# Two small buffers requested first and one mask padded, in a four-branch encoder trunk on one core

## The chip, the cores and the metric

The kernel runs on one core of one Trainium2 chip. The metric is device time in microseconds, lower is better: 2187.64 us before the change, the median of 3 runs (2186.35 to 2188.82).

## The reference

Two inputs of 512 rows by 1024 channels, a prompt and a sample, go independently through the same trunk of two layers. One layer, cut to what matters:

```python
xn = _rms_norm(x, norm_g)
h = xn @ w_in                                   # 1024 -> 8096 columns
h_a, h_b, h_c, h_d, z, mg = _split_cols(h, [A_IN, B_IN, C_IN, D_IN, GATE_IN, MERGE_IN])
ys = [_mla_mixer(h_a, ...), _axial_gqa_mixer(h_b, ...), _sink_window_mixer(h_c, ...), _dilated_mixer(h_d, ...)]
merged = jnp.zeros_like(x)
for i in range(4):
    yi = ys[i] * jax.nn.silu(z[..., i * 256:(i + 1) * 256])
    gi = jax.nn.sigmoid(mg[..., i * D_MODEL:(i + 1) * D_MODEL])
    merged = merged + gi * (yi @ w_branch[i])
return x + merged @ w_out
```

The four mixers are a latent attention (A) and a grouped-query attention (B), both over all 512 positions, a window attention (C) and a dilated one (D). A last RMSNorm ends the trunk. Everything is in float32.

## The kernel before

**Layout of the work.** Activations lie channel-major: a tile has 128 partitions (channels) and a row of T = 512 float32 values (positions), 2048 bytes, in each partition. Four passes run one after the other: layer 0 for prompt and sample, then layer 1 for both. In each pass TensorE multiplies weight tiles of 128x128, which it loads (the page's PEld), by activation tiles, which it streams: a matmul "mm<-xn,wh 128x512" streams one 512-value row of each partition of a tile `xn` against weights of `wh`.

**Three products for one.** Each float32 operand is split in a high part (a rounded copy made on ScalarE) and a low part (the difference, made on VectorE). `mm3` (lines 121 to 124) issues three matmuls: weights high by activation high, high by low, low by high. `project` (line 126) does that over the eight tiles of 128 channels, 24 matmuls for one output tile. The normalised input is in eight buffers `xn0` to `xn7`, the gated branch outputs in `y`, and the queries, keys, latents and the scaled merged sum in `qk`; each of these holds the high row and behind it the low row, 2 x 2048 bytes. `ph` holds a high or a low part of the softmax weights, 2048 bytes. Weights arrive in `wr` and are split into `wh` and `wl` by `piece` (lines 99 to 119).

**Stages of a pass.** The list `steps` sets the program's order: dilated branch D, latents, gate projections `G`, the heads of A, projections and heads of B, branch D's merge `BR`, window branch C, then the merges `M` of A, B and C (each 24 matmuls that stream `xn` and 6 that stream `y` for one output tile). Last comes the output projection with `wo`, which streams eight `qk` tiles (`ms`): 192 matmuls of 128x512 in each of the first three passes, and the same in halves of 256 columns in the fourth. A planner that walks the program with its own clock orders the instructions of each engine, so that matmuls of the merges stand between those of the attention heads.

**Where buffers lie.** All of SBUF's buffers come from one pool through `new(tag, ...)` (line 39). A tag has `bufs` slots; the first request of a tag reserves them, directly behind the tag requested before it, each rounded up to a multiple of 32 bytes. The region begins at byte 16512 of each partition, which is 128 past a multiple of 256. The offsets in the program before the change follow by adding up the sizes in the order of the first requests:

| tags in order of first request | bytes each, slots | first byte | beyond a multiple of 256 |
|---|---|---|---|
| `ident`, `vecs`, `ones`, `heads` | 512, 256, 512, 512 | 16512 | 128 |
| `ms` | 64 x 2 | 18304 | 128 |
| `s`, `wr`, `wh`, `wl` | 8192 x 2, 2560 x 3, x 4, x 4 | 18432 | 0 |
| `qk` | 4096 x 8 | 62976 | 0 |
| `rx`, `rs`, `cos`, `sin`, `rstd` | 2048 x 2, x 3, 2048, 2048, 64 x 4 | 95744 | 0 |
| `nw` | 64 x 2 | 110336 | 0 |
| `lr`, `u` | 2048 x 2, x 2 | 110464 | 128 |
| `xn0` to `xn7` | 4096 each | 118656 | 128 |
| `bcos`, `bsin`, `atab`, `band`, `tri`, `band4` | 2048 x 3, 1536 x 2, 512 | 151424 | 128 |
| `blk` | 128 | 161152 | 128 |
| `v`, `th`, `z`, `mr`, `yf` | 2048 x 4, x 2, x 2, x 4, x 1 | 161280 | 0 |
| `ph` | 2048 x 6 | 187904 | 0 |
| `rc` | 64 x 2 | 200192 | 0 |
| `y` | 4096 x 3 | 200320 | 128 |
| `mg4` to `mg7`, `mg0` to `mg3` | 2048 each | 212608 | 128 |

`nw` is the scratch of the reciprocal square root (`rsqrt`, line 142), `rc` that of the softmax denominators (`gate`, line 301), and `blk` is the smallest mask of the dilated branch, 32 columns, loaded once in `load_tabs` (line 93) and read in `dilated_pair` (line 460). `ident` is streamed by the transposes of `flip` (line 268).

Of the kernel before, what the change touches and what calls it, by code (L numbers as in the profile page):

```python
# [7 lines left out]
F32 = mybir.dt.float32  # L8
# [5 lines left out]
P = 128  # L14
# [14 lines left out]
def trunk(ctx, tc, x0, x1, wp, wr, wu, wg, wb, wm, wo, vec, rope, msk, eye, y0, y1):  # L29
# [9 lines left out]
    def new(tag, shape, dt=F32, bufs=1):  # L39
        uid[0] += 1  # L40
        return sb.tile(shape, dt, tag=tag, name=f"{tag}_{uid[0]}", bufs=bufs)

    def bank(tag, bufs):
        uid[0] += 1
        return pp.tile([P, T], F32, tag=tag, name=f"{tag}_{uid[0]}", bufs=bufs)
# [15 lines left out]


    ident = new("ident", [P, P])
    vecs = new("vecs", [P, vec.shape[1]])

    def vcol(l, j):
        c = l * 24 + j
        return vecs[:, c : c + 1]

    ones = new("ones", [P, P])  # L70
    nc.vector.memset(ones, 1.0)
    heads = new("heads", [P, P])
# [4 lines left out]
    tabs = {}  # L77

    def load_tabs(names=None):
        for n, name in enumerate(("cos", "sin", "bcos", "bsin", "atab")):  # L80
            if name not in tabs and (names is None or name in names):
                tabs[name] = new(name, [P, T])
                nc.sync.dma_start(out=tabs[name], in_=rope[n])
        if names is not None:
            return
        nc.sync.dma_start(out=ident, in_=eye)
        tabs["band"] = new("band", [P, 384])
        nc.sync.dma_start(out=tabs["band"], in_=msk[:, 0:384])
        tabs["tri"] = new("tri", [P, 384])
        nc.sync.dma_start(out=tabs["tri"], in_=msk[:, 384:768])  # L90
        tabs["band4"] = new("band4", [P, P])
        nc.sync.dma_start(out=tabs["band4"], in_=msk[:, 768:896])
        tabs["blk"] = new("blk", [P, 32])
        nc.sync.dma_start(out=tabs["blk"], in_=msk[:, 896:928])


# [438 lines left out]
    def begin(xin):  # L535

        nc.scalar.dma_start(out=vecs, in_=vec)
        warm = new("ms", [P, 16], F32, 2)
        act(out=warm, in_=ones[:, 0:16], func=AF.Exp)
        src = wp[0, T_D + 6 * 1]  # L540
        early = [new("s", [P, 4 * T], F32, 2) for _ in range(2)]
        xt = [early[k // 4][:, (k % 4) * T : (k % 4 + 1) * T] for k in range(NK)]
        xg, pieces, acc = [], [], None
        for k in range(NK):
            nc.sync.dma_start(out=xt[k], in_=xin[:, k, :])
            if k % 4 == 0:
                pieces.append(piece(src[k // 4], 512))
            x = new("qk", [P, 2, T], F32R, 8)
            act(out=x[:, 0, :], in_=xt[k], func=AF.Copy, scale=vcol(0, k))
            stt(out=x[:, 1, :], in0=xt[k], scalar=vcol(0, k), in1=f(x[:, 0, :]), op0=ALU.mult, op1=ALU.subtract)  # L550
            xg.append(x)
            acc = squares(acc, xt[k], k)
        load_tabs(("cos", "sin"))
        bc = rstd([acc], ones, DM, "lr")
        ct, st = new("u", [P, T], F32, 2), new("u", [P, T], F32, 2)
        xn = normalise(0, xt, bc, True)
        tt(out=ct, in0=tabs["cos"], in1=bc, op=ALU.mult)
        tt(out=st, in0=tabs["sin"], in1=bc, op=ALU.mult)
        return xn, (xg, pieces, ct, st, bc)

    def layer(l, q_, xin, last_out, xn, ahead, early=None):
# [12 lines left out]
        def proj_d(g):  # L574
            nonlocal early
            xg, pieces, ct, st_, bc = early or (xn, None, tabs["cos"], tabs["sin"], None)
            p0 = ptile(T_D + 6 * g, xg, pieces)
            p1, p2 = [ptile(T_D + 6 * g + n, xg) for n in (1, 2)] if early else [None, None]
            if early:
                load_tabs()  # L580
            qs = [pack_q(rotary(p0, (0, P), ct, st_))]
            x = rotary(p1 or ptile(T_D + 6 * g + 1), (0, P), ct, st_)
            k1 = pack_k(x, 0, True)
            k4 = pack_k(x, 64)
            ps = p2 or ptile(T_D + 6 * g + 2)
            vt = new("rs", [P, T], F32, 3)
            if early:
                tt(out=inner(vt[64:128]), in0=blocks(ps[64:128]), in1=blocks(bc[64:128]), op=ALU.mult)
            else:
                nc.scalar.copy(out=inner(vt[64:128]), in_=blocks(ps[64:128]))  # L590
            x = rotary(ps, (0, 64), ct, st_)
            early = None
            k16 = pack_k(x, 0)
            v1 = pack_v(flip(vt, (64, 128)))
            qs.append(pack_q(rotary(ptile(T_D + 6 * g + 3), (0, P), tabs["cos"], tabs["sin"])))
            qs.append(pack_q(rotary(ptile(T_D + 6 * g + 4), (0, P), tabs["cos"], tabs["sin"])))
            ps = ptile(T_D + 6 * g + 5)
            vt = new("rs", [P, T], F32, 3)
            nc.scalar.copy(out=vt, in_=ps)
            vp = flip(vt, (0, P))  # L600
            v4 = pack_v(vp[:, :, 0:64])
            v16 = pack_v(vp[:, :, 64:128])
            return qs, [k1, k4, k16], [v1, v4, v16]
# [383 lines left out]
```

## Time and profile before

| | before |
|---|---|
| median of 3 runs | 2187.64 us |
| the profiled execution's own time | 2186.45 us |
| its span, first to last instruction | 2184.7 us |
| mean granted TensorE clock | 0.985 |
| TensorE busy | 2120.6 us, 97%, 9550 matmuls |
| VectorE busy | 1795.1 us, 82% |
| ScalarE busy | 1280.7 us, 59% |
| GpSimd busy | 411.2 us, 19% |
| weight loads busy (beside the matmuls) | 1722.1 us, 79% |
| DMA | 369.76 MB, 169 GB/s on average |

A group of instructions is told by line, engine, operation, its tiles (output<-inputs, the streamed tile first and the weights second) and its shape. The duration of a matmul runs from its start until its last result is out; the next one begins before that. How fast TensorE really goes is therefore read from the distance between the starts of two matmuls that follow each other, and not from the durations. The timeline gives these starts to 0.01 us.

### The profile page before, as it was taken

To read this page: it belongs to the slowest core of one execution; us is meant where nothing else is said; L and a number is where in the kernel's file an instruction comes from. 1 tells how busy PE (TensorE), PEld (TensorE's weight loads), DVE (VectorE), ACT (ScalarE), POOL (GpSimd) and SP (SyncE) were. 2 spreads that over 40 slices of the span, in tenths; PEclk is the share of its full clock that TensorE was granted. 3 is DMA by queue.
4 is the path that set the end of the run, shared out by engine and by line. 5 is a ranking of instruction groups with operands and counts; after the bars stand their busy time and mean duration, and the time that the engine had idled before them with its cause. 6 is when DMAs were issued, how large, how long until landed. Compare 5 with 4: busy or idle time off the path is not lost.

```text
span 2184.7 us, 28862 instructions
## 1 busy us (share of the span) xinstructions
PE 2120.6 (97%) x9550; PEld 1722.1 (79%) x9550; DVE 1795.1 (82%) x3113; ACT 1280.7 (59%) x2167; POOL 411.2 (19%) x145
## 2 busy tenths in 40 slices
PE   7999999999999999999999998999899999999998
PEld 5887778878888778888888776888688887788887
DVE  8999999987478998785379999999866889997725
ACT  6746675444565767553366466754456757675434
POOL 0032313220013221220002222122200232122200
PEclk9999999999999999999999999999899999999999
DMA  6543444556754445556754434455466544455565
GB/s 213 169 145 120 141 141 163 175 186 210 240 165 145 139 138 159 162 191 212 245 179 155 139 117 134 156 166 177 161 226 223 152 152 135 145 158 164 179 207 185
DMA packets 189798, 369.76 MB, mean 169 GB/s; under 512 B 21328, under 2 KB 30032, under 8 KB 188880
## 3 DMA queue, kind: packets, MB, share of 16 engines
q1 hardware_dynamic: 181152, 351.11, 50.0%
q10 hardware_dynamic: 8496, 16.81, 2.3%
q8 instruction: 75, 1.23, 0.2%
q14 instruction: 75, 0.61, 0.1%
HBM read 273.99 MB, written 93.85 MB: 168 GB/s over the span
## 4 chain that ended last, share of the span: by engine, by line
PE 88%; DVE 8%; issue 1%; DMA 1%; ACT 1%; SPq 0%; DVEq 0%; ACTq 0%
PE mm L122 26%; PE mm L123 26%; PE mm L124 25%; PE so L343 1%; PE so L342 1%; PE ss L351 1%; DVE ph L140 1%; PE ss L352 1%; DMA s<-x 1%; DVE wl L115 1%; PE mi L268 1%; PE ss L124 1%; PE ss L123 1%; PE ss L447 1%; PE ss L122 1%
## 5 line engine op out<-in xcount | busy, mean ns | idle before, releaser
L123 PE MATMUL mm<-xn,wh 128*128 128x512 f32 x1992 | 788.5, 396 | 5.9 <-DVE xn L524 5.9
L122 PE MATMUL mm<-xn,wh 128*128 128x512 f32 x1992 | 791.3, 397 | 1.4 <-ACT xn L523 1.0
L124 PE MATMUL mm<-xn,wl 128*128 128x512 f32 x1992 | 788.7, 396 | 0.0
L110 ACT CAST wh<-wr 128x512 fp32r<-128x512 f32 (+1 forms) x596 | 387.1, 651 | 412.5 <-PE mm L123 302.0
L123 PEld LDWEIGHTS mm<-xn,wh 128*128 128x128 f32 x1992 | 376.3, 189 | 90.7 <-DVE xn L524 6.2
L122 PEld LDWEIGHTS mm<-xn,wh 128*128 128x128 f32 x1992 | 376.0, 189 | 88.8 <-ACT xn L523 1.4
L124 PEld LDWEIGHTS mm<-xn,wl 128*128 128x128 f32 x1992 | 376.1, 189 | 85.8 <-issue 1.0
L291 POOL PARTITION_ALL_REDUCE mr<-mr x64 | 239.2, 3737 | 512.2 <-DVE mr L347 265.8
L286 POOL PARTITION_ALL_REDUCE mr<-mr x64 | 129.8, 2029 | 985.3 <-DVE mr L470 577.5
L115 DVE TENSOR_TENSOR wl<-wr,wh 128x512 fp32r<-128x512 f32 (+2 forms) x304 | 247.2, 815 | 40.2 <-ACT wh L110 36.5
L140 DVE TENSOR_TENSOR ph<-s,ph 128x512 fp32r<-128x512 f32 (+2 forms) x256 | 184.9, 729 | 18.6 <-ACT ph L139 10.3
L139 ACT CAST ph<-s 128x512 fp32r<-128x512 f32 (+2 forms) x256 | 144.8, 577 | 30.6 <-PE so L490 11.0
L210 ACT COPY rs<-mm 32x512 f32<-32x512 f32 x240 | 138.8, 578 | 24.5 <-DVE rx L205 19.2
L713 DVE SCALAR_TENSOR_TENSOR th<-th,mm 128x512 f32<-128x512 f32 x96 | 65.4, 681 | 85.7 <-PE mm L124 83.5
L712 ACT ACTIVATE th<-mm 128x512 f32<-128x512 f32 x96 | 57.5, 599 | 132.2 <-PE mm L124 122.6
L122 PE MATMUL mm<-y,wh 128*128 128x512 f32 x256 | 105.1, 414 | 25.1 <-DVE mg L735 13.7
L122 PE MATMUL mm<-qk,wh 128*128 128x512 f32 (+1 forms) x328 | 122.4, 378 | 6.7 <-ACT wh L110 6.2
L124 PE MATMUL mm<-qk,wl 128*128 128x512 f32 (+1 forms) x328 | 122.3, 376 | 0.5 <-DVE wl L115 0.5
L123 PE MATMUL mm<-qk,wh 128*128 128x512 f32 (+1 forms) x328 | 122.3, 376 | 0.3 <-DVE qk L550 0.3
L124 PE MATMUL mm<-y,wl 128*128 128x512 f32 x256 | 104.4, 408 | 0.0
L123 PE MATMUL mm<-y,wh 128*128 128x512 f32 x256 | 104.1, 407 | 0.0
L327 ACT ACTIVATE s<-ss 128x512 f32<-128x512 f32 x128 | 72.3, 597 | 41.0 <-DVE ph L140 22.3
(182 smaller groups left out, 3247.3 us busy)
## 6 DMA issues: line engine op xcount, KB each, us to landing
wr<-wp SPq DMA_DIRECT2D x248, 256.0 KB, 2.8
wr<-wm SPq DMA_DIRECT2D x192, 320.0 KB, 3.2
lo_wp<-wl SPq DMA_DIRECT2D x124, 256.0 KB, 2.0
wl<-lo_wp SPq DMA_DIRECT2D x124, 256.0 KB, 2.7
lo_wm<-wl SPq DMA_DIRECT2D x96, 320.0 KB, 2.2
wl<-lo_wm SPq DMA_DIRECT2D x96, 320.0 KB, 2.9
wr<-wo SPq DMA_DIRECT2D x68, 256.0 KB, 3.6
wr<-wg SPq DMA_DIRECT2D x64, 256.0 KB, 2.8
```

The source lines that it names most:

```text
L110: nc.scalar.copy(out=hi[:, :n], in_=raw[:, :n])
L115: tt(out=lo[:, :n], in0=raw[:, :n], in1=f(hi[:, :n]), op=ALU.subtract)
L122: mm(ps, wh, xh, start=first, stop=False)
L123: mm(ps, wh, xl, start=False, stop=False)
L124: mm(ps, wl, xh, start=False, stop=last)
L139: nc.scalar.copy(out=hi, in_=src)
L140: tt(out=lo, in0=src, in1=f(hi), op=ALU.subtract)
L210: nc.scalar.copy(out=xs[c : c + 32], in_=ps[o : o + 32])
L286: nc.gpsimd.partition_all_reduce(m, t, P, RED.max)
L291: nc.gpsimd.partition_all_reduce(s, t, P, RED.add)
L327: act(out=s[:, j * T : (j + 1) * T], in_=ps, func=AF.Copy, scale=scale)
L713: stt(out=th, in0=th, scalar=1.0, in1=pb, op0=ALU.add, op1=ALU.mult)
```

## The change

Two requests, for `nw` and `rc` with the sizes they had, are made right behind the definition of `new`, so that the first slots of the region are theirs: 2 x 64 and 2 x 64 bytes. The tiles that these two requests return are not used. `blk` becomes a buffer of 64 columns, of which the first 32 are used. Nothing else changes.

```diff
--- before.py
+++ after.py
@@ -39,6 +39,10 @@
     def new(tag, shape, dt=F32, bufs=1):
         uid[0] += 1
         return sb.tile(shape, dt, tag=tag, name=f"{tag}_{uid[0]}", bufs=bufs)
+
+
+    new("nw", [P, 16], F32, 2)
+    new("rc", [P, 16], F32, 2)
 
     def bank(tag, bufs):
         uid[0] += 1
@@ -90,7 +94,7 @@
         nc.sync.dma_start(out=tabs["tri"], in_=msk[:, 384:768])
         tabs["band4"] = new("band4", [P, P])
         nc.sync.dma_start(out=tabs["band4"], in_=msk[:, 768:896])
-        tabs["blk"] = new("blk", [P, 32])
+        tabs["blk"] = new("blk", [P, 64])[:, :32]
         nc.sync.dma_start(out=tabs["blk"], in_=msk[:, 896:928])
 
 
```

By the same sum of sizes, `ident` to `ms` begin 256 bytes later (still 128 beyond a multiple of 256), `s` to `rstd` 256 bytes later (0 beyond), `lr` at 110592, `xn0` at 118784, `blk` at 161280, `v` at 161536, `ph` at 188160, `y` at 200448 and `mg4` at 212736: all these are multiples of 256. Where a matmul streams part of a row (the windows of C and D), its start within the row is what it was.

## The prediction

> **What bounds the kernel now.** First the page: engines, slices, chain.
>
> ```profile
> span 2184.7 us, 28862 instructions
> ...
> PE 2120.6 (97%) x9550; PEld 1722.1 (79%) x9550; DVE 1795.1 (82%) x3113; ACT 1280.7 (59%) x2167; POOL 411.2 (19%) x145
> ...
> PE   7999999999999999999999998999899999999998
> ...
> DVE  8999999987478998785379999999866889997725
> ...
> PE 88%; DVE 8%; issue 1%; DMA 1%; ACT 1%; SPq 0%; DVEq 0%; ACTq 0%
> ```
>
> TensorE is busy nearly everywhere and has 88% of the chain, so a matmul that starts its successor sooner shortens the run, except where VectorE is full as well. The profiled execution took 2186.45 us, 1.75 us more than its span, and 1.2 us less than the median of 2187.64 us; the sum below goes on the median.
>
> Next, which rows are streamed, from the groups kept apart by shape:
>
> ```profile
> L122 PE MATMUL mm<-xn,wh 128*128 128x512 f32 x1992 | 791.3, 397 | 1.4 <-ACT xn L523 1.0 <-DVE mg L735 0.4
> L122 PE MATMUL mm<-y,wh 128*128 128x512 f32 x256 | 105.1, 414 | 25.1 <-DVE mg L735 13.7 <-ACT y L139 11.4
> L122 PE MATMUL mm<-qk,wh 128*128 128x512 f32 x264 | 104.5, 401 | 6.7 <-ACT wh L110 6.2 <-DVE z L318 0.5
> L343 PE MATMUL so<-ph,v 128*128 128x512 f32 x128 | 51.3, 401 | 1.5 <-DVE ph L140 1.5
> L352 PE MATMUL ss<-qk,qk 128*128 128x512 f32 x64 | 24.6, 394 | 0.0
> L656 PE MATMUL mm<-xn,wh 128*128 128x512 f32 x64 | 16.8, 396 | 0.0
> ```
>
> Lines 122 to 124 have the same counts, so 3 x 1992 + 3 x 256 + 64 = 6808 matmuls stream `xn` or `y`, which lie 128 bytes beyond a multiple of 256. 3 x 264 = 792 stream `qk` on a multiple; so do the heads' matmuls (`ph`, and `qk` as scores). The before therefore holds both cases side by side.
>
> The means in these rows mix in waits. What decides is the distance between starts in long stretches without any other matmul. Twice the timeline of TensorE, first the output projection (streams `qk`), then the gate projections of the next pass (stream `xn`), each with its first and last row:
>
> ```profile
> 534.92 0.39 PE L124 MATMUL mm<-qk,wl 128*128 128x512 f32 x1
> ...
> 549.88 0.39 PE L124 MATMUL mm<-qk,wl 128*128 128x512 f32 x1
> ```
>
> ```profile
> 566.67 0.40 PE L123 MATMUL mm<-xn,wh 128*128 128x512 f32 x1
> ...
> 581.85 0.39 PE L122 MATMUL mm<-xn,wh 128*128 128x512 f32 x1
> ```
>
> The first answer has 67 matmuls: 14.96 us over 66 distances, 226.7 ns. The second has 66: 15.18 over 65, 233.5 ns. In a third stretch the order of rows is that of `mm3`:
>
> ```profile
> 145.08 0.39 PE L122 MATMUL mm<-xn,wh 128*128 128x512 f32 x1
> ...
> 158.79 0.40 PE L124 MATMUL mm<-xn,wl 128*128 128x512 f32 x1
> ```
>
> 60 matmuls, 13.71 us over 59 distances: 232.4 ns. Is the neighbourhood the reason? The same two stretches by stage, the granted clock in the third column from the right, DMA share behind it:
>
> ```profile
> 535.00:550.00 15.00, 15.00 (x68) 1.00 0.94 324
> ```
>
> ```profile
> 566.70:581.70 15.00, 15.00 (x66) 1.00 0.75 207
> ```
>
> ```profile
> 535.00:550.00 15.00, 5.52 (x10) 1.00 0.94 324
> ```
>
> ```profile
> 566.70:581.70 15.00, 5.18 (x8) 1.00 0.75 207
> ```
>
> (The last two are VectorE's.) The clock is 1.00 in both, VectorE has 5.5 and 5.2 us of 15, and the transfers are denser in the faster stretch. Weights come from `wh` and `wl` in both. What is left is the streamed tile: its start against 256, or its place.
>
> **The change part by part.** *Instructions.* The two requests and the padding issue nothing: no instruction, transfer or wait is added, and I expect 28862 again. No queue is passed by anything. The unused tiles have no reader that a later slot would have to wait for. Price 0.
>
> *The streamed rows, gross.* 6808 matmuls from 232.4 to 226.7 ns, 5.7 each: 38.8 us. Bounds for one: 0 (the place counts, not the start) and 6.8 (233.5 to 226.7). I take 5.7 because nearly all of them run in the order of the third stretch, with new weights for each.
>
> *What settling costs.* Aligned rows do not run at 226.7 at once. The beginning of another output projection:
>
> ```profile
> 1047.61 0.40 PE L122 MATMUL mm<-qk,wh 128*128 128x512 f32 x1
> ...
> 1050.15 0.39 PE L124 MATMUL mm<-qk,wl 128*128 128x512 f32 x1
> ```
>
> The first 11 distances take 2.54 us, 230.9 each, 46 ns more in all than 11 at 226.7. Such a settling follows, I assume, wherever a stretch is broken by another shape. Those come in packs:
>
> ```profile
> 102.44 1.09 PE L447 MATMUL ss<-qk,qk 128*128 128x512 f32 x4
> ```
>
> ```profile
> L490 PE MATMUL so<-ph,v 128*128 128x128 f32 x128 | 29.8, 271 | 0.4 <-ACT ph L139 0.4
> L495 PE MATMUL so<-ph,v 128*128 128x256 f32 x64 | 12.0, 297 | 0.0
> L268 PE MATMUL mi<-ident,rs 128*128 128x128 f32 x64 | 10.3, 272 | 0.0
> ```
>
> By the same list about 870 matmuls of the attention stages have other shapes (lines 268, 351, 352, 388, 389, 419, 420, 490 to 500). At four to a pack, as in the row of line 447, some 220, to which I add 30 for waits: 250 breaks x 46 ns = 11.5 us. Bounds: 0, and 1570 breaks (every matmul of the heads alone) x 25 ns, a settling cut short, 39 us, which would eat the gross; I take 11.5, since the packs are what the timeline shows.
>
> *The heads' own rows.* 256 of `so` and some 400 of `ss` with 512 columns start on a multiple already, yet their rows show 394 and 401 ns like `xn`; I take it that this is because each stands among unaligned ones. With aligned neighbours they may settle too: 0 to 650 x 4.5 = 3 us; I take 1.5. Matmuls of 64 to 384 columns, and `ident`, which stays 128 beyond: 0.
>
> *Other engines on moved buffers.* VectorE writing `xn` (today 128 beyond) and `mr` (on a multiple today):
>
> ```profile
> L524 DVE TENSOR_TENSOR xn<-s,xn 128x512 fp32r<-128x512 f32 x32 | 20.7, 686 | 0.3 <-ACT xn L523 0.3
> L467 DVE TENSOR_TENSOR mr<-s 128x512 f32<-128x512 f32 x32 | 21.2, 681 | 0.1
> ```
>
> 5 ns apart: over some 500 such instructions 2.5 us either way, hidden under TensorE; 0.
>
> *What VectorE doesn't let through.* Three stages, by engine (PE, PEld, DVE, ACT, POOL):
>
> ```profile
> 150.00:400.00 250.00, 240.58 (x1040) 190.28 (x1039) 247.07 (x404) 159.57 (x267) 65.01 (x20) 0.99 0.45 145
> 850.00:1090.00 240.00, 240.00 (x1057) 196.53 (x1056) 160.40 (x271) 117.60 (x198) 42.08 (x16) 1.00 0.61 197
> 1225.00:1425.00 200.00, 189.81 (x812) 149.43 (x811) 195.61 (x320) 130.96 (x219) 45.20 (x16) 0.97 0.42 136
> ```
>
> In the middle one VectorE idles 79.6 us of 240: whatever TensorE saves counts. In the other two, the heads of A in passes one and three, VectorE idles 2.9 and 4.4 us. Their share of the net so far (38.8 - 11.5 + 1.5 = 28.8) is 450/2185, 5.9 us; between 0 and all of it is lost in waits of `so` and `ss` for `ph` and `s`, which are what is late next there. I take 3.
>
> Sum: 38.8 - 11.5 + 1.5 - 3 = 25.8 us; 2187.6 - 25.8 = 2161.8. **Forecast: 2162 us, 1.2% faster.**
>
> The Trainium skill speaks against this price. "TensorE: Matmul & The Clock Gate" (section "Wait — 56ns, not 53.3ns?") gives starts of 512-column matmuls 215.7 ns apart at full clock, a cost that depends on the columns alone. The trace agrees with neither of its two: 226.7 and 232.4 at clock 1.00. If aligned rows reached that figure, the gain would be an estimated 6808 x 16.7 = 114 us; no row here comes near it.
>
> **The rivals.**
>
> *One: the period is 512, not 256.* Today's `qk` starts on multiples of 512 (62976 = 123 x 512). After the change `xn` does (118784 = 232 x 512), but `qk`, `ph` and `y` lie 256 beyond. Then 5976 + 64 matmuls gain 34.4 us, `qk`'s 792 lose 4.5, `y` stays; less 11.5 and 3: 15.4 saved, 2172. For it: no row in the trace streams from 256 beyond. Against it: nothing but that a half period is the rarer case.
>
> *Two: TensorE's gain is absorbed.* VectorE has 9 in nearly half of its slices. If every stretch where it is above 92% absorbs (about 800 of 2185 us, estimated from the slices), 37% of 28.8 is lost instead of 3: 18 saved, 2169.5. Against: those slices hold gaps in which VectorE itself waits for matmuls.
>
> *Three: the start doesn't matter.* `qk` is faster for its place or its stage, and the change does nothing that counts: 2187.6. For it: the fast stretches of length are all the output projection. Against: the heads of A stream `qk` as well, amid busy engines:
>
> ```profile
> 712.64 0.39 PE L124 MATMUL mm<-qk,wl 128*128 128x512 f32 x1
> ...
> 714.00 0.39 PE L124 MATMUL mm<-qk,wl 128*128 128x512 f32 x1
> ```
>
> Six distances in 1.36 us, 226.7 ns there too; the place of `qk` is then all that could be meant. The Trainium skill is on this side: "SBUF — State Buffer" (section "Door 1: The DMA port swizzle (why `[64,N]` ≈ `[32,N]`)") speaks of lines of 16 bytes as the unit of access, and both starts are multiples of 16; by that rule nothing changes.
>
> *Four: slower.* What counts is the streamed row's start against that of the weights. Today `qk` and `wh` agree modulo 512 and `xn` stands 384 off, `y` 128. Afterwards `y` and `qk` agree with `wh` and `xn` stands 256 off, a case the trace doesn't show. `y` gains 768 x 5.7 = 4.4 us; if `xn` rose by more than 0.7 ns (4.4/6040) the run is slower. At the 233.5 of the second stretch plainly so: 6040 x 1.1 = 6.6, so 2190; were it as far above 232.4 as 226.7 is below, 6040 x 5.7 - 4.4 = 30, 2218. I take 2200. Against: it needs two accesses to meet in just this way.
>
> **How the numbers follow.** Forecast 0.70, one 0.10, two 0.10, three 0.05, four 0.05. The likeliest one's own range: no breaks, no loss and all of the heads, 38.8 + 3 = 42, 2146; breaks twice as dear and the two stages lost, 38.8 - 23 - 3 = 13, 2175. One and two lie inside it; three and four are left out, with the tail of the middle. The range is 2147 to 2174. About 0.2% (4.4 us) can be told from no change here. Faster: forecast, one and two, 0.90; within it: three, 0.05; slower: four, 0.05.
>
> **What would show each step.** The same two stretches: 226.7 in both if the start counts. The gate projections at 232 to 233.5 refute it; then `y` and `qk` tell: both changed with `xn` at 226.7 means one, `xn` above 233.5 means four. The output projection going to 232 means one. Settling: distances above 230 right behind packs only. Absorption: TensorE's busy time falls by much less than its matmuls save, with new idle time before `so` and `ss` in 150 to 400. An order of instructions other than today's would make the sum worthless, since all terms assume it.

## The result and the profile after

| | before | after |
|---|---|---|
| median of 4 runs each | 2186.99 us | 2164.76 us |
| after / before | | 0.9897, 95% interval 0.9882 to 0.9913 |
| the profiled execution's span | 2184.7 us | 2163.3 us |
| TensorE busy | 2120.6 us | 2093.8 us |
| VectorE busy | 1795.1 us | 1795.3 us |
| mean granted TensorE clock | 0.985 | 0.983 |

The run is 22.2 us shorter, 1.0%. The page of the changed kernel (the lines of `mm3` are 126 to 128 there, four more than before):

```profile
span 2163.3 us, 28862 instructions
...
PE 2093.8 (97%) x9550; PEld 1720.4 (80%) x9550; DVE 1795.3 (83%) x3113; ACT 1276.8 (59%) x2167; POOL 412.3 (19%) x145
...
PE 90%; DVE 7%; issue 1%; DMA 1%; ACT 1%; DVEq 0%; SPq 0%; ACTq 0%
...
L126 PE MATMUL mm<-xn,wh 128*128 128x512 f32 x1992 | 782.1, 393 | 2.2 <-ACT xn L527 2.2
L127 PE MATMUL mm<-xn,wh 128*128 128x512 f32 x1992 | 779.5, 391 | 4.7 <-DVE xn L528 4.7
```

The number of instructions is the same, TensorE, VectorE and GpSimd run theirs in the same order, and VectorE's work is unchanged. What is shorter is above all the matmuls that stream `xn`. The timeline of TensorE in the two stretches that the prediction compared, first the output projection (`qk`), then the gate projections (`xn`):

```profile
530.62 0.39 PE L128 MATMUL mm<-qk,wl 128*128 128x512 f32 x1
...
545.58 0.39 PE L128 MATMUL mm<-qk,wl 128*128 128x512 f32 x1
```

```profile
562.13 0.39 PE L126 MATMUL mm<-xn,wh 128*128 128x512 f32 x1
...
577.09 0.39 PE L126 MATMUL mm<-xn,wh 128*128 128x512 f32 x1
```

Each answer has 67 matmuls: 14.96 us over 66 distances in both, 226.7 ns. The gate projections stood at 233.5 before.

By stage the gain is very uneven. These windows of the changed kernel begin and end with the same matmuls as the windows 150 to 400, 790 to 850, 850 to 1090 and 1225 to 1425 of the kernel before (engines PE, PEld, DVE, ACT, POOL, then granted clock, DMA share, GB/s):

```profile
149.66:397.68 248.02, 237.38 (x1041) 189.54 (x1040) 245.08 (x401) 158.74 (x267) 64.98 (x20) 0.99 0.45 146
782.09:842.79 60.70, 57.03 (x241) 45.48 (x240) 52.89 (x89) 42.63 (x74) 12.10 (x5) 0.97 0.52 158
842.79:1078.59 235.80, 235.80 (x1056) 195.99 (x1055) 160.11 (x271) 117.56 (x199) 42.26 (x16) 1.00 0.62 200
1211.50:1411.60 200.10, 190.47 (x812) 152.01 (x811) 194.91 (x319) 130.66 (x219) 44.48 (x16) 0.94 0.41 136
```

The stage in which VectorE has slack goes from 240 to 235.8 us, 1.75%. The heads of A in the first pass go from 250 to 248.0, those of the third pass from 200 to 200.1, with VectorE full in both (245.1 of 248.0, 194.9 of 200.1); the 60 us from 790 on even become 60.7. In the heads of the third pass the granted clock fell from 0.97 to 0.94. Over the whole run, the group whose idle time grew most is the one that waits for the low half of the softmax weights, a subtraction of VectorE:

```profile
L347 PE MATMUL so<-ph,v 128*128 128x512 f32 x128 | 52.1, 407 | 5.5 <-DVE ph L144 5.5
```

That was 1.5 us before. A count over the starts of all 9550 matmuls splits the gain. A distance above 300 ns is taken as a wait, by what it exceeds the mean of the others with the same tiles and columns. Then the distances without a wait sum to 34.8 us less (33.2 of it on `xn` and `y`, 2.0 on the heads' own rows), and the waits to 13.8 us more; together 20.9 of the 21.4 us by which the span shrank. Another bound between 250 and 330 ns moves both figures by up to 1 us.

Not all that counts as a wait here is one. In one place of the third pass the two kernels part. Below are a row of the kernel before, then the same matmul and two later ones of the changed kernel, and last the changed kernel's window by engine:

```profile
1344.02 0.50 PE L343 MATMUL so<-ph,v 128*128 128x512 f32 x1 [0.78 <-DVE ph L140]
```

```profile
1330.39 0.50 PE L347 MATMUL so<-ph,v 128*128 128x512 f32 x1 [2.02 <-DVE ph L144]
...
1337.29 0.63 PE L128 MATMUL mm<-y,wl 128*128 128x512 f32 x1
1337.72 0.63 PE L126 MATMUL mm<-y,wh 128*128 128x512 f32 x1
```

```profile
1331.30:1341.50 10.20, 8.58 (x19) 6.27 (x20) 8.93 (x15) 1.60 (x3) 2.20 (x1) 0.50 0.37 122
```

TensorE waits for the subtraction 1.2 us longer, and then the clock granted is 0.50 for 10.2 us, with matmuls some 427 ns apart. The kernel before has no such stretch there. In it 16 distances of 512-column matmuls are 427 ns, 3.2 us more than at 227. Over the whole run there are 107 distances of 420 to 436 ns, 94 before, so some 2.6 of the 13.8 us are time at half the clock and not time without work. What takes the clock away is not shown: the kernel with everything 128 beyond (below) has 6.8 us of it near the same place, the one with the weights alone 128 beyond has none, and each trace is of one execution.

### The profile page after: what moved, and what is told of

It reads as the page before. It is cut to its first block, busy times and chain, and to the rows that moved or that the text cites. A ratio compares the mean times of both kernels' runs of the same rounds, so it can differ in the third digit from the quotient of the medians.

```text
span 2163.3 us, 28862 instructions
## 1 busy us (share of the span) xinstructions
PE 2093.8 (97%) x9550; PEld 1720.4 (80%) x9550; DVE 1795.3 (83%) x3113; ACT 1276.8 (59%) x2167; POOL 412.3 (19%) x145
## 4 chain that ended last, share of the span: by engine, by line
PE 90%; DVE 7%; issue 1%; DMA 1%; ACT 1%; DVEq 0%; SPq 0%; ACTq 0%
PE mm L126 26%; PE mm L127 26%; PE mm L128 26%; PE so L347 1%; PE so L346 1%; PE ss L355 1%; PE ss L356 1%; DVE ph L144 1%; DMA s<-x 1%; DVE wl L119 1%; PE mi L272 1%; PE ss L451 1%; PE mm L660 1%; PE ss L128 1%; PE ss L127 1%
## 5 line engine op out<-in xcount | busy, mean ns | idle before, releaser
L126 PE MATMUL mm<-xn,wh 128*128 128x512 f32 x1992 | 782.1, 393 | 2.2 <-ACT xn L527 2.2
L127 PE MATMUL mm<-xn,wh 128*128 128x512 f32 x1992 | 779.5, 391 | 4.7 <-DVE xn L528 4.7
L128 PE MATMUL mm<-xn,wl 128*128 128x512 f32 x1992 | 779.7, 392 | 0.0
L144 DVE TENSOR_TENSOR ph<-s,ph 128x512 fp32r<-128x512 f32 (+2 forms) x256 | 186.5, 734 | 13.8 <-ACT ph L143 8.1
```

The lines of the kernel that those rows point to most:

```text
L126: mm(ps, wh, xh, start=first, stop=False)
L127: mm(ps, wh, xl, start=False, stop=False)
L128: mm(ps, wl, xh, start=False, stop=last)
L144: tt(out=lo, in0=src, in1=f(hi), op=ALU.subtract)
```

## The experiments

The theory at this point: a matmul starts its successor 5.7 ns sooner where the streamed row begins on a multiple of 256 bytes, and part of that gain goes into waits for VectorE.

**The offsets by themselves.** The trunk is left out; what remains is chains of matmuls over tiles at chosen places. The core of it, shortened:

```python
offs = {k: stream(f"at{k}", 1032) for k in (0, 32, 64, 96, 128, 160, 192, 224)}   # 4128 bytes each
for r in range(3):
    for k in range(8):                       # hi, lo: the weights of 128 columns
        for ww, i in ((hi, 0), (hi, 1), (lo, 0)):
            mm(out, ww, view(i), start=n == 0, stop=n == 71)
```

> Leaves the whole trunk out: chains of 72 matmuls of 128x512 in the order of mm3 (weights high, high, low), each chain streaming one tile that begins 0, 32, ... 224 bytes beyond a multiple of 256 (at0 to at224), or 4 or 16 bytes beyond (by4, by16), with weights on a multiple of 256; mix0 streams an aligned row against weights 128 beyond, both128 has both 128 beyond; row256 streams 8 pieces of 256 bytes, k96 uses 96 rows; same0 and same128 use the same weights again. Theory (the streamed row's start against 256 decides): at0, mix0 settle at 226.7 ns between starts, at32 to at224 and both128 stay at 230 to 234. Rival (start against the weights' start): mix0 at 232, both128 at 226.7. Rival (start against 64 or 32): at64 or at32 at 226.7 too, which at128 in the kernel before already speaks against. Aligned rows in pieces or on 96 rows: no theory, 226.7 if only the start counts.

The timeline of TensorE, one row for each chain of 72 (buffer numbers are left out: `at` is at0, at32, ... at224 in this order, `by` is by4 and by16, `same` is same0 and then same128, `row` is row256, `k` is k96):

```profile
61.93 16.61 PE L82 MATMUL mm<-at,wgt 128*128 128x512 f32 x72 [0.69 <-ACT o L85]
79.23 17.06 PE L82 MATMUL mm<-at,wgt 128*128 128x512 f32 x72 [0.69 <-ACT o L85]
96.98 16.75 PE L82 MATMUL mm<-at,wgt 128*128 128x512 f32 x72 [0.69 <-ACT o L85]
114.42 17.07 PE L82 MATMUL mm<-at,wgt 128*128 128x512 f32 x72 [0.69 <-ACT o L85]
132.18 17.00 PE L82 MATMUL mm<-at,wgt 128*128 128x512 f32 x72 [0.69 <-ACT o L85]
149.86 17.14 PE L82 MATMUL mm<-at,wgt 128*128 128x512 f32 x72 [0.69 <-ACT o L85]
167.69 17.07 PE L82 MATMUL mm<-at,wgt 128*128 128x512 f32 x72 [0.69 <-ACT o L85]
185.44 17.06 PE L82 MATMUL mm<-at,wgt 128*128 128x512 f32 x72 [0.69 <-ACT o L85]
203.19 17.40 PE L82 MATMUL mm<-by,wgt 128*128 128x512 f32 x72 [0.69 <-ACT o L85]
221.28 16.95 PE L82 MATMUL mm<-by,wgt 128*128 128x512 f32 x72 [0.69 <-ACT o L85]
238.92 16.63 PE L82 MATMUL mm<-row,wgt 128*128 128x512 f32 x72 [0.69 <-ACT o L85]
256.24 16.61 PE L82 MATMUL mm<-k,wgt 96*128 96x512 f32 x72 [0.69 <-ACT o L85]
273.54 16.61 PE L82 MATMUL mm<-same,wgt 128*128 128x512 f32 x72 [0.69 <-ACT o L85]
290.84 17.00 PE L82 MATMUL mm<-mix,wgt 128*128 128x512 f32 x72 [0.69 <-ACT o L85]
308.52 17.00 PE L82 MATMUL mm<-same,wgt 128*128 128x512 f32 x72 [0.69 <-ACT o L85]
326.21 16.64 PE L82 MATMUL mm<-both,wgt 128*128 128x512 f32 x72 [0.69 <-ACT o L85]
```

Against weights on a multiple of 256, only the row that begins on one takes 16.61 us for 72; 32 to 224 beyond take 16.75 to 17.14, 16 bytes beyond 16.95, 4 bytes beyond 17.40. Settled, the last 48 distances of a chain, that is 226.7 ns at 0, 228.9 at 64, 232.4 at 128, 233.3 to 234.3 at the others of 32, 231.7 at 16, and 238.2 at 4. Pieces of 256 bytes (`row`) and 96 rows (`k`) settle like the rest.

The theory falls on the two rows that tell it from its rival. `mix`, an aligned row against weights 128 beyond, takes 17.00; `both`, where row and weights are 128 beyond, takes 16.64. Not the row's own start counts, but **its start against that of the weights**, modulo 256. No other engine works meanwhile. Seven microseconds of the slow `mix` chain by engine (PE, PEld, ACT, POOL, clock, DMA share, GB/s):

```profile
300.00:307.00 7.00, 7.00 (x32) 5.68 (x31) 0.00 (x0) 0.00 (x0) 1.00 0.00 0
```

So it is no contention with another engine or a transfer. (A result is written out only in the first microseconds of a chain.)

**All of it 128 beyond.** The same question in the whole kernel:

```diff
+    new("shift", [P, 32], F32, 1)
     new("nw", [P, 16], F32, 2)
     new("rc", [P, 16], F32, 2)
```

> The full change, and 128 bytes more ahead of it all: every large buffer, the weights wh and wl too, lies 128 beyond a multiple of 256, and all stand against each other as after the change. Theory (start against 256): no stream settles any more, the output projection's 226.7 ns becomes 232 as well: 3 to 5 us slower than before, 2190 to 2192 us. Rival (streamed row against weights): as after the change, 2165 us.

2166.82 us, ratio to before 0.991 (0.9896 to 0.9923): the rival's time, as after the change, though no large buffer begins on a multiple of 256. The output projection in its timeline:

```profile
1059.63 0.39 PE L127 MATMUL mm<-qk,wh 128*128 128x512 f32 x1
...
1075.95 0.39 PE L127 MATMUL mm<-qk,wh 128*128 128x512 f32 x1
```

73 matmuls, 16.32 us over 72 distances, 226.7 ns. Only differences between places count, so the rule does not hang on the byte at which the region begins.

**Only the weights 128 beyond.** The opposite: every streamed row as after the change, on its multiple of 256.

```diff
     new("rc", [P, 16], F32, 2)
+    new("wh", [P, 640], F32R, 4)
+    new("wl", [P, 640], F32R, 4)
```

> The change as it is, except that wh and wl, the weights, are requested at the front as well and so lie 128 beyond a multiple of 256; every streamed row (xn, y, qk, ph) lies where it was to lie after the change, on a multiple of 256. Theory now (the streamed row's start against the weights' start, modulo 256): xn, y and qk all run at 231 to 234 ns, the output projection's 226.7 is lost too, 3 to 6 us slower than before, 2189 to 2193 us. Rival (the streamed row's own start against 256, which the run with all buffers 128 off has spoken against): as after the change, 2165 us.

2190.33 us, ratio 1.0018 (1.0008 to 1.0027): the whole gain is gone, and a little more. The output projection, which no other placement had slowed:

```profile
1059.75 0.39 PE L130 MATMUL mm<-qk,wl 128*128 128x512 f32 x1
...
1075.79 0.39 PE L128 MATMUL mm<-qk,wh 128*128 128x512 f32 x1
```

70 matmuls, 16.04 us over 69 distances: 232.5 ns. With this the rule for a steady offset is settled in the kernel, from both sides. A period of 512 can be told from one of 256, too: after the change `xn0` begins 297 x 256 bytes behind `wh`, an odd multiple, and `y` 616 x 256, an even one; their distances are 227.7 and 227.8 ns, waits aside, so the period is not 512.

**Each half alone.** First only the requests at the front (the mask stays 32 wide), then only the padded mask.

```diff
-        tabs["blk"] = new("blk", [P, 64])[:, :32]
+        tabs["blk"] = new("blk", [P, 32])
```

> Only the two requests moved to the front; the mask stays 32 columns wide. xn0 to xn7 begin on a multiple of 256, but v, ph, y and mg lie 128 beyond. Theory: the 6040 matmuls on xn give 29 of the 34 us that the matmuls gain after the full change, less some 13 of new waits: 16 to 20 us saved, 2167 to 2171 us. Rival (a break by an unaligned neighbour undoes the settling of the rest): half of it, 8 to 12 saved.

2175.12 us, ratio 0.9942 (0.993 to 0.9955): 11.5 us saved, where the theory had 16 to 20 and its rival 8 to 12: the rival's range. `xn` comes down to 228.4 to 228.9 ns (waits aside) instead of 227.7, and `y`, now alone with its offset, stays at 228 to 235 by line. The distances without a wait gain 23.1 us instead of 34.8, while the waits grow by 12.5, almost as much as before. So rows that are off cost those around them as well: the padding, which moves `y` and `ph`, is worth 10 us once `xn` agrees with the weights. The heads' `so` matmuls show the same. Their rows (`ph`) and weights (`v`) agree in every layout, yet they are 231.6 ns apart before the change, 227.5 after it, 231.2 here and 231.8 with the weights `wh` and `wl` 128 beyond: they follow their neighbours.

```diff
-    new("nw", [P, 16], F32, 2)
-    new("rc", [P, 16], F32, 2)
```

> Only the mask padded; the two requests stay where they were. xn stays 128 beyond, y moves onto a multiple of 256, v and ph move to 128 beyond. Theory: the 768 matmuls on y stand between those on xn and settle little: 0 to 4 us saved, 2183 to 2187 us. Rival (the mask or the placement of v and ph counts): outside of that.

2185.01 us, ratio 0.9992 (0.9983 to 1.0001). Without `xn` the padding does nothing that can be told from zero.

**Does VectorE take the rest?** Two kernels with the same work left out, one in the layout before, one after. Each dense head streams the high part of the softmax weights twice and computes no low part, so that TensorE has the same work and VectorE less:

```diff
-            ph, pl = halves(w)
+            ph = new("ph", [P, T], F32R, 6)
+            nc.scalar.copy(out=ph, in_=w)
             mm(o, v[:, j, :], ph, start=j == 0, stop=False)
-            mm(o, v[:, j, :], pl, start=False, stop=j == 3)
+            mm(o, v[:, j, :], ph, start=False, stop=j == 3)
```

> The kernel before, with work of VectorE left out: in the dense heads (A and B) the low parts of the softmax weights are not computed, and their matmuls stream the high parts a second time. TensorE's work is the same, VectorE has 64 subtractions of 128x512 less, some 47 us. It is the base for the next run. Theory (VectorE bounds the heads of A): 8 to 25 us faster than before, 2162 to 2179 us. Rival (VectorE doesn't bound): 2185 to 2187.

> The kernel after the change with the same work left out as in the run ahead of it. Theory (the 13 us that the change lost went into waits for VectorE in the dense heads): the gap to the lean before is 27 to 33 us in place of 21 to 22, most of the 34 us that the matmuls gain. Rival (the loss comes from elsewhere: clock, transfers, start and joints): the gap stays 20 to 23 us.

The expectation counted 64 subtractions; there are 128, and VectorE's busy time is 73 us less (the page of the lean kernel before). The lean kernel before is 26 us faster than the full one, just beyond the 8 to 25 expected:

```profile
PE 2113.4 (98%) x9550; PEld 1716.2 (79%) x9550; DVE 1721.7 (80%) x2985; ACT 1278.5 (59%) x2167; POOL 398.2 (18%) x145
```

2160.87 and 2133.56 us. In the lean kernels the change is worth 27.3 us instead of 22.2, the lower edge of the theory's range. The distances without a wait gain 35.0 there, about as much as in the full kernel, and the waits grow by 8.8 instead of 13.8. So with the lean heads some 5 us less of the gain is held back; each of the two gains is known to about 3 us, so the size is rough. That VectorE's time does it is likely but not separated: a lean head also asks for half as many `ph` buffers, and the planner orders the lean kernels' matmuls otherwise. Of the other 8.8 us, 2.4 are again time at half the clock (71 distances of 420 to 436 ns instead of 59); the rest stays open.

**Two attempts to give VectorE room.** The sums of the softmax weights on GpSimd:

```diff
-        tt(out=t, in0=s[:, 0:T], in1=s[:, T : 2 * T], op=ALU.add)
+        nc.gpsimd.tensor_tensor(out=t, in0=s[:, 0:T], in1=s[:, T : 2 * T], op=ALU.add)
         for j in (2, 3):
-            tt(out=t, in0=t, in1=s[:, j * T : (j + 1) * T], op=ALU.add)
+            nc.gpsimd.tensor_tensor(out=t, in0=t, in1=s[:, j * T : (j + 1) * T], op=ALU.add)
```

> The kernel after the change, with the three additions per dense head that sum the softmax weights over the key blocks moved from VectorE to GpSimd; nothing is left out. VectorE has 48 additions of 128x512 less, some 33 us, mostly in the heads' stages. Theory (VectorE bounds there): 4 to 12 us faster than after the change, 2153 to 2161 us. Rival (GpSimd is slow at additions, or holds up VectorE's own): 0 to 15 us slower than after the change.

2346.74 us, ratio 1.0731 (1.0716 to 1.0745), far outside of both expectations. GpSimd's groups:

```profile
L351 POOL TENSOR_TENSOR mr<-mr,s 128x512 f32<-128x512 f32 x64 | 100.0, 1563 | 5.8 <-ACT s L341 1.0
L349 POOL TENSOR_TENSOR mr<-s 128x512 f32<-128x512 f32 x32 | 51.4, 1607 | 230.4 <-ACT ph L143 115.5 <-ACT s L341 44.4 <-ACT wh L114 34.3
```

There are 96 additions (the expectation said 48), at 1.6 us each, 0.7 on VectorE. They stand on the queue of the all-reduces which every softmax needs; 151 us of additions, 182 us lost against the change. The group of the all-reduce that follows a head's sums shows a larger item:

```profile
L295 POOL PARTITION_ALL_REDUCE mr<-mr x64 | 218.4, 3412 | 394.6 <-issue 198.7 <-DVE mr L408 129.4 <-DVE mr L474 65.7
```

After the sums of each of the 32 heads GpSimd idles 6.2 us before the all-reduce starts, 198.7 us in all, for nothing that the profile shows, and ScalarE waits 151.9 us for these all-reduces; after the change the group has no such idle time and ScalarE waits 31.4 us. The trace has 130 instructions MODIFY_POOL_CONFIG on GpSimd, 64 each at the lines of the first addition and of this all-reduce, against 2 after the change. So the switch between additions and all-reduces is the likelier price than the additions themselves. Neither it nor the order of the queue was tried apart.

Then one of two equal subtractions in `pack_k` as a copy on ScalarE:

```diff
-        tt(out=inner(k[a : a + 64, 1 - own, :], near), in0=src, in1=f(hi), op=ALU.subtract)
+        nc.scalar.copy(out=k[a : a + 64, 1 - own, :], in_=f(k[o : o + 64, own, :]))
```

> The change, and in pack_k the second of two equal subtractions on VectorE becomes a copy of the first one's result on ScalarE: 40 times 64x512, 0.7 us each, 28 us less on VectorE and 25 more on ScalarE, in the projections of D, B and C; nothing is left out. Theory (waits for VectorE take back part of the gain): 1 to 5 us faster than after the change, 2160 to 2164 us. Rival (those stages have slack, and the copy stands behind a subtraction it must wait for): 0 to 4 us slower, 2165 to 2169.

2179.96 us, ratio 0.9979 (0.9969 to 0.9989): 15 us slower than the change alone, again outside. The 40 subtractions are gone with their 28 us, but VectorE's busy time falls by 9 us only, since its other instructions take longer:

```profile
PE 2096.8 (96%) x9550; PEld 1723.1 (79%) x9550; DVE 1785.9 (82%) x3073; ACT 1302.6 (60%) x2207; POOL 415.3 (19%) x145
```

TensorE's busy time is 3 us above that after the change and the span 13.7 us, so it is mostly waits. The planner orders the engines' work anew for such an edit; whether the copy itself or that order costs the time stays open. No version tried, of those that compute all, beats the change.

**Whose weights?** While a row streams, the weights of the next matmul are being loaded: in these traces a load of 0.19 us starts within 0.01 us of each matmul's start. The next run has chains in which weights alternate between 0 and 128 beyond (`wt`, `wm_`), and in which the row agrees with its own weights or with the next ones:

```python
chain((wt, wm_), (pair0, both), 0)      # tiles same0, both128: row n agrees with weights n
chain((wt, wm_), (mix, pair1), 1)       # tiles mix0, same128: row n agrees with weights n + 1
chain((wt, wm_), (low,), 0)             # tile k96: the row stays, weights alternate
```

> Leaves the whole trunk out; chains of 72 matmuls of 128x512 as in the run with the offsets, each run twice. The streams at (on 256, then 128 beyond) have weights on 256 throughout: 226.7 and 232.4 ns. In the next chain weights alternate between 0 and 128 beyond, and the stream alternates with them (same0 for even, both128 for odd): each row agrees with the weights it is multiplied by, and not with the weights of the next matmul, which are loaded while it streams. In the one after (mix0, same128) it is the other way round: each row agrees with the next matmul's weights and not with its own. In the last, weights alternate and the row stays (k96). Theory (a row and the load of the next weights, which run at the same time, disturb one another unless their starts agree modulo 256): same0/both128 at 230 to 235 ns, mix0/same128 at 226.7, k96 in between or unsettled. Rival (the row against its own weights): same0/both128 at 226.7, mix0/same128 at 230 to 235. Neither, when both are unsettled: then only a steady offset settles.

The timeline, first and last of 51 rows of either chain:

```profile
102.33 0.39 PE L76 MATMUL mm<-both,wgt 128*128 128x512 f32 x1
...
113.74 0.40 PE L76 MATMUL mm<-both,wgt 128*128 128x512 f32 x1
```

```profile
119.77 0.39 PE L76 MATMUL mm<-mix,wgt 128*128 128x512 f32 x1
...
131.27 0.40 PE L76 MATMUL mm<-mix,wgt 128*128 128x512 f32 x1
```

228.2 ns where a row agrees with its own weights, 230.0 with the next ones, 232.2 where the row stays and the weights alternate. Neither theory's 226.7 appears. Agreement with the own weights comes nearest, but no simple rule follows: in the last chain, too, each row agrees either with its own weights or with the next ones, in turn, and it is as slow as a steady 128. What in the chip makes the two starts disturb one another is open; only the rule for a steady offset stands.

## Why the prediction was right, and where not

The time, 2162 forecast and 2165 measured, came out. Two of the steps behind it are off in size, and the reason given is not the right one.

- **Nothing added:** right. 28862 instructions, the same order on TensorE, VectorE and GpSimd.
- **The streamed rows, 5.7 ns each, 38.8 us gross:** right in size. Settled stretches went from 233.5 to 226.7, and the distances on `xn`, waits aside, from 232.5 to 227.7 on average.
- **Why:** wrong. The step put the price on the row's own start against 256. Before the change the weights lay on a multiple of 256, so that the trace could not tell the row's own start from its start against the weights. The runs with everything, and with the weights alone, 128 beyond gave 2167 and 2190. The fourth rival had the mechanism, but with a period of 512, and concluded slower from it; with 256 the same mechanism gives the forecast's gain. That the wrong reason gave the right price was luck of this layout: by the rule that the runs show, moving the rows would have gained nothing with weights 128 beyond, as the 2190 shows. "What is left is the streamed tile" left out the other tile that TensorE reads.
- **Settling, 11.5 us:** over-priced. `xn` and `y` gained 33.2 of the 38.8, which leaves 5.6 for settling. In the chains a row on its place reaches 226 to 227 after four to nine distances behind the restart, 21 to 46 ns in all; 46 was the dear end.
- **The heads' own rows, 1.5 us:** 2.0, and for the reason given, the neighbours.
- **Other engines, 0:** right, VectorE 1795.1 and 1795.3 us.
- **What VectorE doesn't let through, 3 us:** the term that failed. The waits grew by 13.8. The step looked at two stages, put their share at 5.9 and took half. There 5.2 of 7.2 us were lost: about half in the first pass, all in the third. The larger part lies in places it had not counted. Between 790 and 850 the stage lost 0.7 us outright, and the corresponding stretch of the fourth pass 0.9, though VectorE was busy 86 and 94% there before the change; the waits of these two grew by 4.0 us. And the step had no term for the clock: more time at half the clock is 2.6 of the 13.8.

38.8 - 5.6 + 2.0 - 13.8 = 21.4; all other rows lost 0.4, which makes it 21.0. The errors of settling (6 too dear) and of the waits (11 too cheap) half cancelled.

- **Rivals one and three** (period 512; the start doesn't matter): refuted by 226.7 in both stretches. **Rival two** (VectorE absorbs) holds in part: it named the mechanism and put 11 us on it, nearer to the 13.8 than the forecast's 3; but it looked for it above 92% only, and it had no clock either.

## What to carry to other kernels

For float32 matmuls that follow one another closely, place the streamed rows and the weight tiles at the same offset modulo 256 bytes; here it is 5.7 ns of 232, 2.5% of each settled 512-column matmul with a weight tile of its own, and it costs three lines. Other column counts and types were not tried apart. One misplaced buffer ahead of the others shifts all behind it, and streams that are off spoil their neighbours, so check every buffer that TensorE reads, weights included. When TensorE gets faster, look for its waits stage by stage, also where the other engine is not full, and look at the granted clock: of 35 us of shorter distances 14 were lost again here, nearly 3 of them at half the clock.

## What the runs showed of the hardware that was not expected

- The distance between matmuls depends on two operands' places together: 226.7 ns at equal offsets, 228.9 at 64 apart, 232.4 at 128, 233.3 to 234.3 at the other multiples of 32, 231.7 at 16 bytes, 238.2 at 4, with no other engine at work.
- It is not a fixed surcharge per matmul. A steady offset of 128 repeats a pattern of seven distances from 228 to 241 ns, and a row on its place needs four to nine distances behind a restart until all are 226 or 227. Matmuls whose own row and weights agree stay near 231 to 232 among others that do not.
- An addition of 128x512 took 1.56 to 1.61 us on GpSimd on average, 0.68 on VectorE, and GpSimd idled 6.2 us between such additions and the next all-reduce.
